# Overflow check and the rows of the last normalisation in the last unit but one, least-used experts last but one

## Chip, core and metric

The kernel runs on one core of a Trainium2 chip. The metric is the device time of one execution in microseconds (us). Engines are named as in the profile: PE (matmul), PEld (weight load of PE), DVE (vector), ACT (scalar), POOL, SP (issues nearly all transfers).

## The reference

Two layers, each a token-mixing part and then a hierarchical mixture of experts, for 256 tokens of width 1024. The part that the change touches, cut to its core:

```python
def hier_moe(h, w_grp, b_grp, w_rt, b_rt, w_gate, w_up, w_down):
    ...
    g_idx = jnp.argmax(grp_logits, axis=-1)
    ...
    top_v, top_i = lax.top_k(sel, TOP_K_IN_GROUP)
    ...
    for e in range(N_EXPERTS):
        a = jax.nn.silu(t @ w_gate[e]) * (t @ w_up[e])
        out = out + combine[:, e:e + 1] * (a @ w_down[e])
...
for l in range(DEPTH):
    ...
    x = layer_norm(DEEPNORM_ALPHA * x + (1 + gt1) * mix, ln1_g[l], ln1_b[l])
    h = x * (1 + sc2) + sh2
    ffn = hier_moe(h, ...)
    x = layer_norm(DEEPNORM_ALPHA * x + (1 + gt2) * ffn, ln2_g[l], ln2_b[l])
```

There are 32 experts of three matrices, each 1024 x 512 in 32-bit floats. Every token goes to two of them. For the inputs used here the reference's router gives these token counts: in layer 0, experts 4 to 31 in falling order 40, 40, 37, 34, 28, 28, 25, 22, 22, 20, 18, 15, 14, 11, 10, 10, 9, 8, 7, 6, 5, 5, 4, 3, 2, 1, 0, 0; in layer 1, 62, 53, 51, 37, 31, 27, 23, 21, 20, 19, 19, 17, 14, 13, 12, 10, 9, 7, 5, 4, 3, 3, 3, 3, 3, 2, 2, 0. So two experts of layer 0 and one of layer 1 have no token.

## The kernel before

**The ring of weights.** All large weights stream through 18 slots of 1 MiB (`RING`). `stream` is the list of loads in the order in which they are used; `pump` issues the next load on SP when one of the 18 is given back, and `done` gives slots back after the matmuls that read them. The order is fixed when the program is written; SP runs ahead of PE by at most 18 slots.

**Places and units.** Experts 0 to 3 stand at places 0 to 3. The other 28 are sorted by their token count on the device, and places 4 to 31 hold them in falling order. Places 0 to 11 get room for 64 tokens each and are worked on in pairs (units 0 to 5), places 12 to 31 get room for 32 each and are worked on in fours (units 6 to 10). A unit of four has 24 loads of 1 MiB: 8 for gate, 8 for up, 8 for down, and within each the four experts alternate. The load of an expert at a place from 4 on has a condition (L176), true where it has at least one token; a load whose condition is false moves no bytes, but holds its slot like any other until PE has passed it. PE does the matmuls of such an expert all the same, on what lies in the slot, and the result is multiplied by zero.

Line 53 makes the units of four in the order 28-31, 24-27, 20-23, 16-19, 12-15, so the four places with fewest tokens are unit 6 and places 12 to 15 are the last unit:

```python
UNITS += [[(p0 + j, 32 * j, 32) for j in range(4)] for p0 in range(NE - 4, FIXED + WIDE - 1, -4)]
```

**A unit on PE** (`experts`, from L1061): gate matmuls (L1117), on every second unit the gathering of the tokens of the next two (`gather`, L1096), up matmuls (L1117), the adding of the unit before to the result `y` in PSUM (`scatter`, L1126), transposes (L1183, L1139), down matmuls (L1205). After the last unit but one (`i == NU - 2`) `add_x` adds the residual to `y` (L1133).

**The overflow check.** `spill` (L1232) handles the case in which an expert has more tokens than its place has room for. Each of the five engines loads the largest overflow from SBUF into a register (L1233) and branches (L1234). Where nothing overflows, as with these inputs, each jumps over the body and its semaphores are stepped on; instructions behind the check that wait for an engine's work wait for that step too (L1234 in the profile). The check stands behind `experts`, at the end of each layer.

**The end of a layer.** Layer 0 is followed by the front of layer 1: `gate_sum` on PE (L387, L479) with the four loads of a gate matrix, `normalise_psum` on DVE and ACT (L546 to L565), transposes of X (L572), and the first section of the projection (L593) with two loads. Layer 1 is followed by the last normalisation (from L1316): PE spreads its scale and shift rows (`fing`, `finb`) over the partitions (L387), ACT copies the scale (L1324), DVE centres and scales (L1337), applies the reciprocal deviation and adds the shift (L1346), and four transfers write the result.

Of the kernel before, what the change touches and what calls it, by code (L numbers as in the profile page):

```python
# [8 lines left out]
F32 = mybir.dt.float32  # L9
BF16 = mybir.dt.bfloat16  # L10
# [17 lines left out]
def kernel(  # L28
# [21 lines left out]

    NR = NE - FIXED
    UNITS = [[(p0 + j, 64 * j, 64) for j in range(2)] for p0 in range(0, FIXED + WIDE, 2)]
    UNITS += [[(p0 + j, 32 * j, 32) for j in range(4)] for p0 in range(NE - 4, FIXED + WIDE - 1, -4)]
    NU = len(UNITS)
    NQ = (NU + 1) // 2
    H = 4
# [1000 lines left out]
        return gc, bc, Xp, posm, rest, places, gsum  # L1057


    def experts(l, gc, bc, Xp, posm, rest, places, gsum, mp):  # L1060
        Gs, Ws, XTs = {}, {}, {}  # L1061
        parts = Xp.bitcast(BF16).rearrange("t k (a c d) -> t a c k d", a=3, c=NTC)
# [46 lines left out]
        wts, eos = {}, {}  # L1109
        st = small.tile([P, NTC, 2, 6], F32, tag="bnst2", name="bnst2")  # L1110

        def proj(i, nm):
# [45 lines left out]
        for i in range(NU):  # L1158
# [69 lines left out]
        ovc, ci = placed["over"]  # L1228
        return y, sts, ovc, ci, gt2


    def spill(l, gc, bc, Xp, ovc, ci, gt, y, sts, mp):  # L1232
        n = nc.values_load(ci[0:1, 0:1], min_val=0, max_val=NT + 32)  # L1233
        with tc.If(n > SLOTS):  # L1234
            for tci in range(NTC):
                for h in range(2):
                    V.tensor_copy(Xn(tci, h), y[tci][h].rearrange("t (p k) -> t p k", k=KD))

            parts = Xp.bitcast(BF16).rearrange("t k (a c d) -> t a c k d", a=3, c=NTC)
            for k in range(KD):  # L1240
                ps = pa.tile([P, 512], F32, tag="a", name="ovh")
                for tci in range(NTC):
                    for a in range(3):
                        T.matmul(ps[:, tci * P:(tci + 1) * P], parts[:, a, tci, k, :], identb,
                                 start=(a == 0), stop=(a == 2))
                S.activation(Xp[:, k, 0:NT], ps[:, 0:NT], AF.Identity, scale=gc[:, k:k + 1], bias=bc[:, k:k + 1])
            with tc.For_i(0, NE, 1) as e:
                for kk in range(KF):
                    f0 = kk * P
                    wg = mp.tile([P, KD, P], F32, tag="XT", name="ovg", bufs=3)  # L1250
                    G.dma_start(wg, w_gate[l][bass.ds(e, 1), :, f0:f0 + P].rearrange(
                        "o (p k) f -> p (o k) f", k=KD))
                    wu = mp.tile([P, KD, P], F32, tag="XT", name="ovu", bufs=3)
                    G.dma_start(wu, w_up[l][bass.ds(e, 1), :, f0:f0 + P].rearrange(
                        "o (p k) f -> p (o k) f", k=KD))
                    wd = mp.tile([P, D], F32, tag="eo", name="ovd", bufs=1)
                    G.dma_start(wd, w_down[l][bass.ds(e, 1), f0:f0 + P, :].rearrange("o p f -> p (o f)"))
                    gps = pa.tile([P, 512], F32, tag="a", name="ovgp")
                    ups = pa.tile([P, 512], F32, tag="a", name="ovup")
                    for ps, w in ((gps, wg), (ups, wu)):  # L1260
                        for k in range(KD):
                            T.matmul(ps[:, 0:NT], w[:, k, :], Xp[:, k, 0:NT], start=(k == 0), stop=(k == KD - 1))
                    aT = mp.tile([P, NT], F32, tag="sg", name="ova", bufs=1)
                    S.activation(aT, gps[:, 0:NT], AF.Silu)
                    V.tensor_tensor(aT, aT, ups[:, 0:NT], op=ALU.mult)
                    for tci in range(NTC):
                        for h in range(2):
                            T.matmul(y[tci][h], aT[:, tci * P:(tci + 1) * P], wd[:, h * 512:(h + 1) * 512],
                                     start=(kk == 0), stop=(kk == KF - 1))
                for tci in range(NTC):  # L1270
                    for h in range(2):
                        t = mp.tile([P, 512], F32, tag="t2", name="ovt")
                        V.tensor_scalar_mul(t, y[tci][h], ovc[:, tci, bass.ds(e, 1)])
                        V.tensor_tensor(t, t, gt[:, h * 512:(h + 1) * 512], op=ALU.mult)
                        xv = Xn(tci, h)
                        V.tensor_tensor(xv, xv, t.rearrange("t (p k) -> t p k", k=KD), op=ALU.add)
            for tci in range(NTC):
                for h in range(2):
                    T.matmul(y[tci][h], ident, Xn(tci, h), start=True, stop=True)
                    V.bn_stats(sts[tci][:, h, :], y[tci][h])  # L1280

    y, sts = None, None
    early, affine = {}, {}
# [2 lines left out]
    for l in range(L):  # L1286
# [24 lines left out]
        fp.stack.close()  # L1311
        mp = moe_pool(l)
        gc, bc, Xp, posm, rest, places, gsum = routing(l, wrs[l], asum, mp)
        y, sts, ovc, ci, gt2 = experts(l, gc, bc, Xp, posm, rest, places, gsum, mp)
        spill(l, gc, bc, Xp, ovc, ci, gt2, y, sts, mp)
        S.preload_act_table_set(LNEXP)  # L1316
        if l + 1 == L:

            fg = mp.tile([P, D], F32, tag="XT", name="fing", bufs=3)
            fb = []  # L1320
            for h in range(2):
# [3 lines left out]
            for h in range(2):  # L1325
# [65 lines left out]
```

## Time and profile before

| | |
|---|---|
| median of 3 executions | 1250.45 us (1249.53 to 1251.41) |
| the profiled execution | 1247.88 us, of which 1246.2 us is the span from first to last instruction |
| mean granted TensorE clock | 0.941 of full |
| PE busy | 1065.2 us, 85% of the span |
| DVE, ACT, POOL busy | 344.8, 172.0, 72.5 us |
| share of the 16 DMA engines taken by SP's queue | 92.7% |
| moved by DMA | 467.62 MB, mean 375 GB/s |

Busy PE is not PE at its peak: matmuls are pipelined and their ends are modelled. Where PE waits for a load, the load is the bound there; where SP waits for PE to give a slot back, PE is. Both occur in this kernel, so the stages have to be read one by one.

### The profile page before, as it was taken

The page shows a single profiled execution, that of the slowest core. Times are in us where ns is not written, and L with a number is a line of the kernel's source. Part 1 is how long each engine was busy: PE and PEld are TensorE (multiplying, and loading weights), DVE is VectorE, ACT ScalarE, POOL GpSimd, SP SyncE. Part 2 cuts the span into 40 slices and gives each one's busy share as a digit, 9 for nine tenths or more (in the row PEclk, how much of TensorE's full clock was granted, in tenths as well). Part 3 has the DMA queues.
Part 4 walks back from the last instruction along what each step waited for, and adds up shares of the span by engine and source line. Part 5 has one row for each costly group of instructions (what it writes and reads, how often), then busy time and mean ns, then how long its engine had stood idle before and what let it go on. Part 6 is the DMA issues. An engine that isn't in the chain of part 4 may idle for free. (4 is left out here: it accounts for less than half of the span.)

```text
span 1246.2 us, 14270 instructions
## 1 busy us (share of the span) xinstructions
PE 1065.2 (85%) x5317; PEld 421.6 (34%) x5320; DVE 344.8 (28%) x801; ACT 172.0 (14%) x403; POOL 72.5 (6%) x52
## 2 busy tenths in 40 slices
PE   5998879899999866788679998989999977677965
PEld 1464434334343311121124653443434221112211
DVE  1386366311121100310034546641112101030103
ACT  1145322101010100000111331310101010000010
POOL 0204520000000000000000301100000000000000
PEclk7999999999999988889989999999999988888897
DMA  9999778899979999999999926889999999999994
GB/s 349 365 411 346 310 297 332 341 403 420 421 312 373 421 422 420 422 421 421 402 395 397 397 70 247 355 343 406 421 421 422 409 421 422 420 422 422 420 409 178
DMA packets 89262, 467.62 MB, mean 375 GB/s; under 512 B 12301, under 2 KB 12817, under 8 KB 40290
## 3 DMA queue, kind: packets, MB, share of 16 engines
q1 hardware_dynamic: 88818, 465.85, 92.7%
q8 instruction: 45, 0.74, 0.2%
q10 hardware_dynamic: 288, 0.52, 0.1%
q0 software_dynamic: 80, 0.26, 0.1%
q14 instruction: 31, 0.25, 0.1%
HBM read 484.43 MB, written 1.05 MB: 390 GB/s over the span
## 5 line engine op out<-in xcount | busy, mean ns | idle before, releaser
L1205 PE MATMUL dps<-w,eaT_moe 128*32 128x512 f32 (+1 forms) x1024 | 199.8, 655 | 39.7 <-DMA w<-in_w_down_dram 30.9
L1117 PE MATMUL up<-w,XT_moe 128*32 128x512 f32 (+1 forms) x1024 | 193.5, 625 | 41.3 <-DMA w<-in_w_up_dram 41.3
L1117 PE MATMUL gate<-w,XT_moe 128*32 128x512 f32 (+1 forms) x1024 | 195.1, 648 | 31.2 <-DMA w<-in_w_gate_dram 31.1
L593 PE MATMUL sec<-w,hT_front 128*128 128x512 f32 x256 | 114.2, 600 | 1.6 <-DVE hT_front L582 1.6
L1205 PEld LDWEIGHTS dps<-w,eaT_moe 128*32 128x32 f32 (+1 forms) x1024 | 53.3, 128 | 169.6 <-issue 100.9
L1117 PEld LDWEIGHTS up<-w,XT_moe 128*32 128x32 f32 (+1 forms) x1024 | 52.2, 124 | 172.3 <-issue 97.4
L1117 PEld LDWEIGHTS gate<-w,XT_moe 128*32 128x32 f32 (+1 forms) x1024 | 53.7, 128 | 167.3 <-issue 107.7
L1171 DVE TENSOR_TENSOR act_moe<-sg_moe,up 128x512 f32<-128x512 f32 x22 | 15.1, 688 | 340.1 <-PE up L1117 340.1
L1211 DVE TENSOR_TENSOR eo_moe<-dps,gt 128x512 f32<-128x512 f32 x44 | 30.4, 691 | 207.0 <-PE dps L1205 207.0
L1126 PE MATMUL y<-eo_moe,wt_moe 128*128 128x512 f32 x176 | 84.9, 607 | 1.6 <-DVE eo_moe L1211 1.6
L1161 ACT ACTIVATE sg_moe<-gate 128x512 f32<-128x512 f32 x22 | 13.1, 597 | 429.2 <-PE gate L1117 429.2
L593 PEld LDWEIGHTS sec<-w,hT_front 128*128 128x128 f32 x256 | 48.0, 192 | 58.5 <-issue 53.3
L1096 PE MATMUL gps<-G_moe,Xp_moe 128*128 128x256 bf16 (+1 forms) x672 | 64.6, 250 | 3.7 <-DVE XT_moe L1102 1.7
L1102 DVE TENSOR_SCALAR XT_moe<-gps,gc,bc 128x128 f32<-128x128 f32 x88 | 30.6, 404 | 126.5 <-PE gps L1096 126.5
L1096 PEld LDWEIGHTS <-Xp_moe 128*128 128x128 bf16 x672 | 53.2, 98 | 21.9 <-issue 13.1
L1141 ACT COPY wt_moe<-wtps 128x256 f32<-128x256 f32 x22 | 8.2, 372 | 287.6 <-PE wtps L1139 287.6
L1126 PEld LDWEIGHTS y<-eo_moe,wt_moe 128*128 128x128 f32 x176 | 30.3, 191 | 43.9 <-issue 40.5
L1105 ACT ACTIVATE XT_moe<-gps,bc,gc 128x128 f32<-128x128 f32 x88 | 33.7, 455 | 42.1 <-PE gps L1096 42.1
L461 POOL TENSOR_TENSOR w<-w,w 128x2048 f32<-128x2048 f32 x7 | 31.6, 4519 | 52.4 <-ACT w L457 41.8
L415 PE MATMUL ada_s<-w,csl 128*32 128x512 f32 x128 | 20.7, 764 | 10.5 <-DMA w<-in_w_ada_dram 10.5
L860 PE MATMUL wo<-w,zu_front 128*128 128x512 f32 x64 | 29.2, 610 | 0.0
L754 PE MATMUL u<-hT_front,w 128*128 128x256 f32 x128 | 28.8, 379 | 0.0
(274 smaller groups left out, 768.6 us busy)
## 6 DMA issues: line engine op xcount, KB each, us to landing
w<-in_w_gate_dram SPq DMA_DIRECT2D x128, 1024.0 KB
w<-in_w_up_dram SPq DMA_DIRECT2D x128, 1024.0 KB
w<-in_w_down_dram SPq DMA_DIRECT2D x120, 1024.0 KB
w<-in_w_ada_dram SPq DMA_DIRECT2D x48, 1024.0 KB
w<-in_w_in_dram SPq DMA_DIRECT2D x20, 1024.0 KB
w<-in_w_out_dram SPq DMA_DIRECT2D x8, 1024.0 KB
w<-in_w_down_dram SPq DMA_DIRECT2D x16, 512.0 KB
xin_front<-in_x_dram SPq DMA_DIRECT2D x2, 512.0 KB
```

Of the source, the lines that this page charges most:

```text
L415: T.matmul(ps[32 * j:32 * j + 32], cs(k), held["ada", l, part, k][:, 0, j * 512:(j + 1) * 512], start=(k == 0), stop=(k == KD - 1))
L461: G.tensor_tensor(acc, acc, w, op=ALU.add)
L593: T.matmul(ps, hT[:, k, tci * P:(tci + 1) * P], held["in", l, s, k // 4][:, k % 4, :], start=(k == 0), stop=(k == KD - 1))
L754: T.matmul(ps[:, 0:NT], held["in", l, U_, k // 4][:, k % 4, g * P:(g + 1) * P], hT[:, k, :], start=(k == 0), stop=(k == KD - 1))
L860: T.matmul(o_ps[tci][h], (cat, zu)[hf][:, kk, tci * P:(tci + 1) * P], w[:, kk, :], start=(hf == 1 and kk == 0), stop=(hf == 0 and kk == 3))
L1096: T.matmul(ps[:, k - kk].rearrange("p j s -> p (j s)"), parts[:, a, tci, k, :], g[:, tci, js[0] * P:(js[-1] + 1) * P], start=(a == 0 and t ...
L1102: V.tensor_scalar(dst, ps[:, k - kk, i, :], gc[:, k:k + 1], bc[:, k:k + 1], op0=ALU.mult, op1=ALU.add)
L1105: S.activation(dst, ps[:, k - kk, i, :], AF.Identity, scale=gc[:, k:k + 1], bias=bc[:, k:k + 1])
L1117: T.matmul(ps[c0:c0 + w], xt[:, k, c0:c0 + w], held[nm, l, place, k // 4][:, k % 4, :], start=(k == 0), stop=(k == KD - 1))
L1126: T.matmul(y[tci][h], wt[:, tci, :], eo[:, h, :], start=(i == 0), stop=(i == NU - 1))
L1205: T.matmul(dps[h][s0:s0 + w], aT[:, kk, s0:s0 + w], held["down", l, place, part][:, kk - ks[0], c0:c0 + 512], start=(kk == 0), stop=(kk == ...
L1211: V.tensor_tensor(eo[:, h, :], dps[h], gt2[:, h * 512:(h + 1) * 512], op=ALU.mult)
```

## The change

Three things are done. The units of four now come in the order 12-15, 16-19, 20-23, 28-31, 24-27. `spill` moves from the end of the layer into the last unit but one, ahead of `add_x`; its body is rewritten so that it adds to the residual X in place of `y`, and it runs only on overflow. The rows of the last normalisation are spread in the last unit but one of layer 1 (`last_rows`), and the shift row is copied to SBUF too; the second preload of the activation table at the layer's end goes.

```diff
-    UNITS += [[(p0 + j, 32 * j, 32) for j in range(4)] for p0 in range(NE - 4, FIXED + WIDE - 1, -4)]
+    FOURS = [[(p0 + j, 32 * j, 32) for j in range(4)] for p0 in range(FIXED + WIDE, NE, 4)]
+    UNITS += FOURS[:-2] + [FOURS[-1], FOURS[-2]]
...
+    def spill(l, gc, bc, Xp, ovc, ci, gt, mp):
+        n = nc.values_load(ci[0:1, 0:1], min_val=0, max_val=NT + 32)
...
+        with tc.If(n > SLOTS):
...
+    def last_rows(l, mp):
+        fg = mp.tile([P, D], F32, tag="XT", name="fing", bufs=3)
+        fb = mp.tile([P, D], F32, tag="Xp", name="finb")
+        for row, r in ((fg, R_LN2G + l), (fb, R_LN2B + l)):
+            for h in range(2):
+                ps = pm.tile([P, 512], F32, tag="m", name="finps")
+                spread(ps, r, h * 512, 512, True, True)
+                (V.tensor_copy if h else S.copy)(row[:, h * 512:(h + 1) * 512], ps)
+        return fg, fb
...
             if i == NU - 2:
+
+                spill(l, gc, bc, Xp, *placed["over"], gt2, mp)
                 add_x()
+                if l + 1 == L:
+                    fin = last_rows(l, mp)
...
-        y, sts, ovc, ci, gt2 = experts(l, gc, bc, Xp, posm, rest, places, gsum, mp)
-        spill(l, gc, bc, Xp, ovc, ci, gt2, y, sts, mp)
-        S.preload_act_table_set(LNEXP)
+        y, sts, fin = experts(l, gc, bc, Xp, posm, rest, places, gsum, mp)
         if l + 1 == L:
 
-            fg = mp.tile([P, D], F32, tag="XT", name="fing", bufs=3)
-            fb = []
-            for h in range(2):
-                ps = pa.tile([P, 512], F32, tag="a", name="fingps")
-                spread(ps, R_LN2G + l, h * 512, 512, True, True)
-                S.copy(fg[:, h * 512:(h + 1) * 512], ps)
-            for h in range(2):
-                fb.append(pm.tile([P, 512], F32, tag="m", name="finbps"))
-                spread(fb[h], R_LN2B + l, h * 512, 512, True, True)
+            fg, fb = fin
...
-                V.scalar_tensor_tensor(o, o, rs[:, tci:tci + 1], fb[h], op0=ALU.mult, op1=ALU.add)
+                V.scalar_tensor_tensor(o, o, rs[:, tci:tci + 1], fb[:, cs], op0=ALU.mult, op1=ALU.add)
```

How this moves instructions is seen at two places. The first is PE at the end of layer 0: the last down matmul and the two last matmuls into `y`, then, in the kernel before, the check with its body (skipped here), and the first matmuls of layer 1 (`gate_g`). Before:

```order
L1205 MATMUL dps<-w_91,eaT_moe_3546 32x512
L1126 MATMUL y_1199<-eo_moe_3553,wt_moe_3551 128x512
L1126 MATMUL y_1201<-eo_moe_3553,wt_moe_3551 128x512
L1233 TENSOR_LOAD ci
L1234 COMPARE_AND_BRANCH
L1244 LDWEIGHTS Xp_moe_1017
...
L1234 UNCONDITIONAL_BRANCH x2
L387 LDWEIGHTS pick_140
L387 MATMUL gate_g_3862<-rw_139,pick_140 32x512
```

The same place with the change:

```order
L1259 MATMUL dps<-w_91,eaT_moe_3789 32x512
L1180 MATMUL y_1199<-eo_moe_3796,wt_moe_3794 128x512
L1180 MATMUL y_1201<-eo_moe_3796,wt_moe_3794 128x512
L388 LDWEIGHTS pick_140
L388 MATMUL gate_g_3861<-rw_139,pick_140 32x512
```

The check has gone from between the two layers. It stands now behind the down matmuls of the last unit but one, on PE ahead of the residual's matmuls and the gate matmuls of the last unit:

```order
L1259 MATMUL dps<-w_95,eaT_moe_3385 32x512
L1062 TENSOR_LOAD ci
L1070 COMPARE_AND_BRANCH
L1076 LDWEIGHTS Xp_moe_1017
...
L1070 UNCONDITIONAL_BRANCH
L1187 MATMUL y_1198<-X,ident 128x512
L1187 MATMUL y_1199<-X,ident 128x512
L1187 MATMUL y_1200<-X,ident 128x512
L1187 MATMUL y_1201<-X,ident 128x512
L1171 MATMUL gate_3694<-w_80,XT_moe_3234 32x512
```

The second place is ACT at the end of layer 1: the end of the check, the copies of the scale row, and the logarithm and exponential that make the reciprocal deviation (`rsy`). Before:

```order
L1247 REGISTER_ALU
L1247 COMPARE_AND_BRANCH
L1247 UNCONDITIONAL_BRANCH
L1234 UNCONDITIONAL_BRANCH x2
L1316 ACT_TABLE_LOAD
L1324 COPY fing_moe_7362<-fingps 128x512 x2
L527 ACTIVATE rsy<-rsv 128x2
L528 ACTIVATE rsy<-rsy 128x2
```

With the change:

```order
L1070 UNCONDITIONAL_BRANCH
L1110 COPY fing_moe_7218<-finps 128x512
L1110 COPY finb_moe_7219<-finps 128x512
L1215 ACTIVATE sg_moe_7273<-gate_7232 128x512
L1195 COPY wt_moe_7326<-wtps 128x256
L1281 ACT_TABLE_LOAD
L528 ACTIVATE rsy<-rsv 128x2
L529 ACTIVATE rsy<-rsy 128x2
```

The copies now stand ahead of the last unit's own two instructions (`sg`, `wt`), and nothing is left between the table and `rsy`. DVE copies the other halves of the two rows at the same place.

## Rows read from the trace of the kernel before

**Rows 1.** The page, GB/s moved in each of 40 slices of 31.2 us

```profile
GB/s 349 365 411 346 310 297 332 341 403 420 421 312 373 421 422 420 422 421 421 402 395 397 397 70 247 355 343 406 421 421 422 409 421 422 420 422 422 420 409 178
```

**Rows 2.** Waits: who waited for what: us in total, times, longest us

```profile
PE dps L1205 <- DMA w<-in_w_down_dram: 30.9, 27, 2.2
```

**Rows 3.** Windows of layer 0: busy, count by engine; PE clock, DMA share, GB/s

```profile
350.00:360.00 10.00, 9.85 (x70) 5.88 (x68) 2.73 (x8) 3.60 (x9) 0.00 (x0) 1.00 1.01 419
360.00:370.00 10.00, 10.00 (x42) 3.98 (x40) 2.14 (x4) 0.37 (x1) 0.00 (x0) 1.00 0.64 246
370.00:380.00 10.00, 10.00 (x74) 3.01 (x74) 1.38 (x2) 0.00 (x0) 0.00 (x0) 1.00 0.43 157
380.00:390.00 10.00, 10.00 (x84) 3.19 (x77) 1.28 (x3) 0.60 (x1) 0.00 (x0) 1.00 0.96 368
...
590.00:600.00 10.00, 8.56 (x48) 2.67 (x44) 0.00 (x0) 0.60 (x1) 0.00 (x0) 1.00 1.01 420
```

**Rows 4.** Timeline of PE in unit 6 of layer 0, and the start of unit 7

```profile
374.56 7.07 PE L1117 MATMUL gate<-w,XT_moe 128*32 128x512 f32 x64
...
392.75 7.07 PE L1205 MATMUL dps<-w,eaT_moe 128*32 128x512 f32 x64
...
405.19 1.04 PE L1117 MATMUL gate<-w,XT_moe 128*32 128x512 f32 x2 [1.10 <-DMA w<-in_w_gate_dram]
```

**Rows 5.** Windows of layer 1 around its unit 6

```profile
960.00:970.00 10.00, 10.00 (x54) 3.32 (x56) 2.51 (x5) 0.37 (x1) 0.00 (x0) 1.00 1.01 397
970.00:980.00 10.00, 10.00 (x99) 2.99 (x92) 0.00 (x0) 0.60 (x1) 0.00 (x0) 1.00 1.00 413
```

**Rows 6.** Timeline of PE in unit 9 of layer 0

```profile
536.40 1.57 PE L1096 MATMUL gps<-G_moe,Xp_moe 128*128 128x128 bf16 x24 [0.15 <-DVE XT_moe L1102]
...
572.77 7.18 PE L1133 MATMUL y<-X,ident 128*128 128x512 f32 x8
```

**Rows 7.** Timeline of all engines where layer 1 follows layer 0

```profile
631.11 1.90 PE L1205 MATMUL dps<-w,eaT_moe 128*32 128x512 f32 x10 [0.30 <-DMA w<-in_w_down_dram]
...
633.79 1.98 PE L1126 MATMUL y<-eo_moe,wt_moe 128*128 128x512 f32 x4 [0.78 <-DVE eo_moe L1211]
...
638.32 0.16 DVE L563 SCALAR_TENSOR_TENSOR nm<-mv,rs 128x1 f32<-128x1 f32 x1
640.60 1.24 ACT L564 ACTIVATE X<-y,nm,rs 128x512 f32<-128x512 f32 x1 [2.95 <-PEq L1234]
...
640.62 0.61 PE L387 MATMUL gate_g<-rw,pick 128*32 128x512 bf16 x2 [4.84 <-PEq L1234]
640.63 4.01 PE L479 MATMUL gate_g<-w,csl 128*32 128x512 f32 x16
...
644.57 1.68 PE L572 MATMUL hTps<-ident,X 128*128 128x128 f32 x8
...
646.17 1.92 PE L479 MATMUL gate_g<-w,csl 128*32 128x512 f32 x16
...
648.03 7.13 PE L593 MATMUL sec<-w,hT_front 128*128 128x512 f32 x16
```

**Rows 8.** Window at the same place, columns as in rows 3

```profile
643.00:644.00 1.00, 1.00 (x8) 0.00 (x0) 0.00 (x0) 0.00 (x0) 0.00 (x0) 0.50 1.10 395
```

**Rows 9.** Timeline of the end of layer 1

```profile
1233.69 0.70 DVE L1226 BATCH_NORM_STATS2 bnst<-y 128x6 f32<-128x512 f32 x1 [0.16 <-PE y L1126]
...
1234.74 0.28 DVE L1330 BATCH_NORM_AGGREGATE fmv<-bnst 128x2 f32<-128x12 f32 x2 [0.36 <-DVEq L1234]
1235.06 0.17 DVE L525 TENSOR_SCALAR rsv<-fmv 128x2 f32<-128x2 f32 x1
...
1236.39 1.07 ACT L1324 COPY fing_moe<-fingps 128x512 f32<-128x512 f32 x2 [20.94 <-PE fingps L387]
...
1237.01 0.75 DVE L1337 SCALAR_TENSOR_TENSOR o_moe<-y,fmv,fing_moe 128x512 f32<-128x512 f32 x1 [1.78 <-ACT fing_moe L1324]
...
1240.28 2.72 DVE L1346 SCALAR_TENSOR_TENSOR o_moe<-o_moe,frs,finbps 128x512 f32<-128x512 f32 x4
```

More of the change, by code (lines that the diff above doesn't have):

```diff
@@ L1057, in routing @@
         return gc, bc, Xp, posm, rest, places, gsum
+    def spill(l, gc, bc, Xp, ovc, ci, gt, mp):
+        n = nc.values_load(ci[0:1, 0:1], min_val=0, max_val=NT + 32)
+        wg = Xp[:, :, NT:NT + P]
+        wu = mp.tile([P, KD, P], F32, tag="XT", name="ovu", bufs=3)
+        wd = [mp.tile([P, 512], F32, tag=tag, name=f"ovd_{tag}", bufs=1) for tag in ("a", "aT")]
+        aT = mp.tile([P, NT], F32, tag="sg", name="ova", bufs=1)
+        t = mp.tile([P, 512], F32, tag="t2", name="ovt")
+        gps, ups = [pa.tile([P, 512], F32, tag="a", name=f"ovp{i}") for i in range(2)]
+        ps = pm.tile([P, 512], F32, tag="m", name="ovps")
+        with tc.If(n > SLOTS):
+            parts = Xp.bitcast(BF16).rearrange("t k (a c d) -> t a c k d", a=3, c=NTC)
+            for k in range(KD):
+                for tci in range(NTC):
+                    for a in range(3):
+                        T.matmul(ps[:, tci * P:(tci + 1) * P], parts[:, a, tci, k, :], identb,
+                                 start=(a == 0), stop=(a == 2))
+                S.activation(Xp[:, k, 0:NT], ps[:, 0:NT], AF.Identity, scale=gc[:, k:k + 1], bias=bc[:, k:k + 1])
+            with tc.For_i(0, NE, 1) as e:
+                for kk in range(KF):
+                    f0 = kk * P
+                    G.dma_start(wg, w_gate[l][bass.ds(e, 1), :, f0:f0 + P].rearrange(
+                        "o (p k) f -> p (o k) f", k=KD))
+                    G.dma_start(wu, w_up[l][bass.ds(e, 1), :, f0:f0 + P].rearrange(
+                        "o (p k) f -> p (o k) f", k=KD))
+                    for h in range(2):
+                        G.dma_start(wd[h], w_down[l][bass.ds(e, 1), f0:f0 + P, h * 512:(h + 1) * 512].rearrange(
+                            "o p f -> p (o f)"))
+                    for pp, w in ((gps, wg), (ups, wu)):
+                        for k in range(KD):
+                            T.matmul(pp[:, 0:NT], w[:, k, :], Xp[:, k, 0:NT], start=(k == 0), stop=(k == KD - 1))
+                    S.activation(aT, gps[:, 0:NT], AF.Silu)
+                    V.tensor_tensor(aT, aT, ups[:, 0:NT], op=ALU.mult)
+                    for tci in range(NTC):
+                        for h in range(2):
+                            T.matmul(ps, aT[:, tci * P:(tci + 1) * P], wd[h], start=True, stop=True)
+                            V.tensor_scalar_mul(t, ps, ovc[:, tci, bass.ds(e, 1)])
+                            V.tensor_tensor(t, t, gt[:, h * 512:(h + 1) * 512], op=ALU.mult)
+                            xv = Xn(tci, h)
+                            V.tensor_tensor(xv, xv, t.rearrange("t (p k) -> t p k", k=KD), op=ALU.add)
@@ L1060, in experts @@
+    def last_rows(l, mp):
+        fg = mp.tile([P, D], F32, tag="XT", name="fing", bufs=3)
+        fb = mp.tile([P, D], F32, tag="Xp", name="finb")
+        for row, r in ((fg, R_LN2G + l), (fb, R_LN2B + l)):
+            for h in range(2):
+                ps = pm.tile([P, 512], F32, tag="m", name="finps")
+                spread(ps, r, h * 512, 512, True, True)
+                (V.tensor_copy if h else S.copy)(row[:, h * 512:(h + 1) * 512], ps)
+        return fg, fb
     def experts(l, gc, bc, Xp, posm, rest, places, gsum, mp):
@@ L1108, in experts @@
         y = [[py.tile([P, 512], F32, tag="s", name=f"y{tci}{h}") for h in range(2)] for tci in range(NTC)]
-        wts, eos = {}, {}
+        wts, eos, fin = {}, {}, None
         st = small.tile([P, NTC, 2, 6], F32, tag="bnst2", name="bnst2")
@@ L1227, in experts @@
         sts = [st[:, tci] for tci in range(NTC)]
[L1228 to L1235, printed above, removed]
-                for h in range(2):
[L1237 to L1266, printed above, removed]
-                        for h in range(2):
[L1268 to L1280, printed above, removed]
@@ L1282 @@
+        return y, sts, fin
     y, sts = None, None
@@ L1313 @@
         gc, bc, Xp, posm, rest, places, gsum = routing(l, wrs[l], asum, mp)
-        y, sts, ovc, ci, gt2 = experts(l, gc, bc, Xp, posm, rest, places, gsum, mp)
-        spill(l, gc, bc, Xp, ovc, ci, gt2, y, sts, mp)
-        S.preload_act_table_set(LNEXP)
+        y, sts, fin = experts(l, gc, bc, Xp, posm, rest, places, gsum, mp)
         if l + 1 == L:
-            fg = mp.tile([P, D], F32, tag="XT", name="fing", bufs=3)
-            fb = []
-            for h in range(2):
-                ps = pa.tile([P, 512], F32, tag="a", name="fingps")
-                spread(ps, R_LN2G + l, h * 512, 512, True, True)
-                S.copy(fg[:, h * 512:(h + 1) * 512], ps)
-            for h in range(2):
-                fb.append(pm.tile([P, 512], F32, tag="m", name="finbps"))
-                spread(fb[h], R_LN2B + l, h * 512, 512, True, True)
+            fg, fb = fin
             mv = small.tile([P, NTC, 2], F32, tag="fmv", name="fmv")
```

## Prediction, before the changed kernel was run

> **What bounds the kernel now.** I read first the GB/s of the 40 slices [rows 1]. The reader is to see a ceiling of 420 to 422 and the slices below it: around slices 12 and 13 (312 and 373, some 343 to 405 us) and in slices 24 to 27. In the ceiling stretches PE waits for loads, for those of down 27 times with 30.9 us in all [rows 2]. So the second half of each layer's experts is bound by the transfers, and what counts there is whether the transfers ever stop. The front of layer 1 (the 70 GB/s slice) is the opposite: the ring is full and PE is the bound. A gain ahead of either kind of stretch is therefore kept only if it moves the resource that binds there, and I take the four places of the change one by one.
>
> Windows of 10 us in layer 0 show the dip closely [rows 3]: 419 GB/s up to 360 us, then 246, 157 and 368, and from 390 us to 600 us, in 21 windows, 417 to 426 (the last is shown). In the dip PE is busy without a break and the granted clock is at its upper level, 2.4 GHz (1.00). PE there is in unit 6 [rows 4]: gate from 374.56, down until 392.75 + 7.07 = 399.8 us, no wait for a load before 405.19. This unit holds the four places with fewest tokens, two of which have none in layer 0. Their 12 loads fill 12 of the 18 slots without giving the transfers anything to do, and PE, which at this time is behind the transfers, has not yet passed them. So the transfers run dry.
>
> **Part 1, the order of the units.** The bytes missing in the dip are (421 - 246) + (421 - 157) + (421 - 368) GB/s over 10 us each, which at 421 GB/s is 4.2 + 6.3 + 1.3 = 11.7 us. By the busy share instead (0.64, 0.43, 0.96 against 1.01) it is 3.7 + 5.7 + 0.5 = 9.9 us. Since the transfers then run at the ceiling until the layer's last load, this is time that layer 0 ends later.
>
> With the change unit 6 is full and the ring holds real loads. Would the stop come back in unit 9? One load takes 1.0486 MB / 421 GB/s = 2.49 us. Unit 9 then has 12 real loads, 29.9 us, and unit 10 has 24, 59.8 us: 89.7 us together. PE needs for a unit of four with all loads there 399.8 - 374.56 = 25.2 us; in unit 9 come the gathering, 2 x 1.57 = 3.1 us, the residual, 7.18 us [rows 6], and the check, 4.84 us [rows 7]: 40.3 us, and 65.5 us for both units. So PE enters unit 9 waiting for loads, ends it 10.4 us late by these sums (40.3 - 29.9), some 20 us with the matmuls that only follow the last loads, and has 24 us of cover until the last load. Twenty us are 8 loads, and SP may run 18 slots ahead, by then all of them loads of unit 10. The transfers do not stop, and I take 11.7 us; lower end 9.9, or nothing in the rival below.
>
> In layer 1 only one expert is empty and the same place loses (421 - 397) + (421 - 413) over 10 us each [rows 5]: 0.8 us, lower end 0.
>
> **Part 2, the check between the layers.** PE's last work of layer 0 is the two matmuls into `y`, over at 633.79 + 1.98 = 635.77 us; the check then holds PE for 4.84 us, to 640.62. ACT and DVE have `nm` at 638.48 but start to normalise X only at 640.60, because they wait for PE's step in the check [rows 7]. So 4.84 us go on PE and 2.12 us on DVE and ACT. But PE, too early, meets the loads. The last load of layer 0 let PE go on at 631.11; at the 395 GB/s shown here [rows 8] one load takes 2.65 us, and between it and the first section stand four loads of the gate matrix, so the section's first load lands at about 631.1 + 5 x 2.65 = 644.4 us. The compute path without the check: X normalised from 638.2 (DVE loses a short wait too) for 1.24 us to 639.5, transposes 1.0 to 1.7 us, the second half of the gate waits for its fourth load (641.7), 1.92 us, done at 642.7 to 643.6. The load comes last: the section starts at 644.4 in place of 648.03, a gain of 3.6 us, on the earlier time base of part 1. From there PE works through the front without waiting for loads, so the gain passes into layer 1's experts, where the ring is refilled by PE's pace.
>
> The clock is the uncertain thing here. Behind the check it is at its lower level, 1.2 GHz (0.50) [rows 8], and 16 matmuls of the gate take 4.01 us; the next 16 take 1.92 us. Without the 4.84 us of idleness it may stay up: that would be worth 2.1 us more, had the loads been there, so the upper end is 4.84 + 2.1 = 6.9 us. PE will instead wait in pieces for loads; if the clock falls during these and the section begins at the lower level, a stretch as long as the one shown costs the 7.13 us section up to 3.6 us, and the lower end is 0. By the Trainium skill ("TensorE: Matmul & The Clock Gate", Part 1) the throttled clock is the default and activity releases it, which would give the upper end's clock where PE stays busy. By that rule the part would be nearer 6.9 us; the transfers keep me at 3.6.
>
> **Part 3, the end of layer 1.** The last statistics end at 1233.69 + 0.70 = 1234.39 us. DVE is ready to centre after `rsv`, 1235.23, and has lost 0.36 us to the check ahead of the aggregate. It then waits for `fing`, copied from 1236.39 on, until 1237.01, and the last scaling starts 3.27 us later at 1240.28 [rows 9]. With rows made in unit 9, `rsv` ends near 1234.9, the first centring starts at about 1234.95, and the logarithm and exponential, which stood behind ACT's copies, fit under it. Gain 1237.01 - 1234.95 = 2.1 us (1.7 if the 0.36 us stay; 2.3 at most). The shift read from SBUF in place of PSUM I leave at no cost.
>
> **Part 4, what is added.** In each layer PE's check stands ahead of the residual and the last unit's gate. Behind it on PE wait the last unit's matmuls, and SP waits for these to give slots back. In layer 1 come four matmuls and four copies for the rows, under 4 us on PE with the waits between them (four copies of 0.54 us, two of them on DVE beside ACT). All this lies in the 24 us of part 1 (39 us in layer 1, whose unit 9 has 18 real loads, 44.8 us), so nothing. Without that cover the check costs 4.84 us in each layer, 9.7 us.
>
> **The sum.** 11.7 + 0.8 + 3.6 + 2.1 = 18.2 us. The profiled execution took 1247.88 us, 1246.2 us of it the span; the median shown is 2.6 us above it, so I subtract from the median: 1250.45 - 18.2 = 1232.3 us.
>
> **Rivals.**
> *The stop returns in unit 9.* The empty experts' slots still fill the ring, now while PE stands in the check and the residual. For it: the cause, 12 empty slots among 24, is the same. Against it: before unit 6 PE never waited for a load, before unit 9 it waits for loads unit after unit, so the slots drain as they are issued. Part 1's 11.7 us would be lost: 1244.0 us.
> *The loads were not the bound, and the front's clock falls.* Only the end of layer 1 and the 0.8 us would remain: 1250.45 - 2.9 = 1247.5 us or a little above. The 21 windows at the ceiling speak against it.
> *Slower: the check stops PE in mid-stream for long.* PE's stop of 4.84 us [rows 7] was measured with the transfers still at about 395 GB/s [rows 8], so the stream alone should not lengthen it. With no cover at all it costs 2 x 4.84 = 9.7 us and gives 1242.0 us. The kernel is slower by more than 0.2% only where the uncovered time passes 18.2 + 2.5 = 20.7 us, some 10.4 us in each layer: with the cover of 24 us that is a stop of nearly 40 us (4.84 + 24 + 10.4), eight times the one shown.
> The Trainium skill ("Runtime: NRT & Kernel Launch", Instruction fetch mechanics) says that a taken branch whose target is not in the fetched window forces a fetch by DMA before execution goes on. By this rule the check stays dear on every engine and DVE, whose skipped body grows, would pay like PE; by the row, DVE paid 0.36 us. Uncovered, the rule gives the 1242.0 us above; covered, it changes nothing.
>
> **Chances.** The forecast 0.76; the stop returns 0.13; next to nothing remains 0.04; the check uncovered 0.07, of which 0.03 slower. Adding ends: best 11.7 + 0.8 + 6.9 + 2.3 = 21.7 gives 1228.7; worst of the forecast 9.9 + 0 + 0 + 1.7 = 11.6 gives 1238.9. To hold 8 in 10 I go from 1228.5 to 1241, into the partial return of the stop. A measurement of this kernel can tell about 0.2%, 2.5 us, from no change. Faster by more than that: 0.92; within it 0.05; slower 0.03.
>
> **What would show it.** Part 1: windows of the changed kernel in layer 0 from some 270 us to the layer's end stay at the ceiling, with no window under 400 before the last 40 us, and the last down load of layer 0 lets PE go on at about 619.4 in place of 631.11. Part 2: PE goes from `y` to the gate without a wait for the check, and the first section waits for its load, and from the last down load's release to the section's first matmul it is 644.4 - 631.1 = 13.3 us in place of 16.9. Part 3: the last scaling starts about 3.8 us after the last statistics in place of 5.9. Wrong would I be if the transfers stop in unit 9, or if PE's waits for the last unit's down loads have gone, which would mean that PE has become the bound.

## The result, and the profile after

With the change the kernel takes 1235.22 us (median; 1234.19 to 1235.47) where before takes 1249.99 us beside it: a ratio of 0.9888, 95% interval 0.9876 to 0.99, that is 14.0 us (12.5 to 15.5) less. Forecast were 18.2 us less, 1232.3 us, with a range of 1228.5 to 1241. The profiled execution took 1234.19 us, its span 1232.6 us.

The GB/s of the 40 slices after, to be held against [rows 1]:

```profile
GB/s 354 365 409 307 294 280 349 347 405 420 422 420 422 421 421 421 421 422 420 400 396 397 388 86 276 348 343 403 422 421 421 420 422 420 421 421 421 420 411 201
```

Slices 12 and 13, which were at 312 and 373, are at the ceiling, and the 409 of layer 1 is 420. The same windows as [rows 3] and [rows 5] (busy and count of PE, PEld, DVE, ACT, POOL; clock, DMA share, GB/s):

```profile
360.00:370.00 10.00, 10.00 (x42) 3.91 (x39) 1.38 (x2) 0.88 (x3) 0.00 (x0) 1.00 1.02 420
370.00:380.00 10.00, 10.00 (x60) 3.16 (x62) 2.15 (x4) 0.37 (x1) 0.00 (x0) 1.00 1.01 420
380.00:390.00 10.00, 8.98 (x82) 2.56 (x74) 0.00 (x0) 0.60 (x1) 0.00 (x0) 1.00 1.01 420
...
550.00:560.00 10.00, 10.00 (x92) 4.05 (x90) 1.42 (x3) 1.34 (x4) 0.00 (x0) 1.00 1.01 419
...
590.00:600.00 10.00, 8.30 (x43) 2.00 (x41) 0.00 (x0) 0.00 (x0) 0.00 (x0) 1.00 1.01 410
...
960.00:970.00 10.00, 9.80 (x82) 2.58 (x74) 0.00 (x0) 0.60 (x1) 0.00 (x0) 1.00 1.02 424
970.00:980.00 10.00, 8.76 (x46) 3.25 (x46) 2.05 (x4) 0.37 (x1) 0.00 (x0) 1.00 1.02 421
```

The stop is gone, and none has come where the unit with the empty experts stands now (550 to 560 us): of the 33 windows from 270 to 600 us the lowest is the 410 shown. PE's timeline there, from the last down matmuls of unit 9 through unit 10 (start, duration, instruction, idle time before it and what ended that), answers to [rows 6]:

```profile
562.67 7.07 PE L1259 MATMUL dps<-w,eaT_moe 128*32 128x512 f32 x64
574.05 7.24 PE L1187 MATMUL y<-X,ident 128*128 128x512 f32 x8 [4.31 <-PEq L1070]
581.22 7.07 PE L1171 MATMUL gate<-w,XT_moe 128*32 128x512 f32 x64
...
598.70 1.04 PE L1171 MATMUL up<-w,XT_moe 128*32 128x512 f32 x2 [1.45 <-DMA w<-in_w_up_dram]
```

The check costs PE 4.31 us here. From 562.67 to 598 us PE then waits for no load, so it is behind the transfers; at 598.70 it waits for one again, so it has caught up. The boundary between the layers, all engines, against [rows 7]:

```profile
622.79 1.90 PE L1259 MATMUL dps<-w,eaT_moe 128*32 128x512 f32 x10 [0.31 <-DMA w<-in_w_down_dram]
...
625.48 1.98 PE L1180 MATMUL y<-eo_moe,wt_moe 128*128 128x512 f32 x4 [0.79 <-DVE eo_moe L1265]
...
627.40 2.10 PE L480 MATMUL gate_g<-w,csl 128*32 128x512 f32 x16
...
629.83 1.21 ACT L565 ACTIVATE X<-y,nm,rs 128x512 f32<-128x512 f32 x1 [0.86 <-DVE nm L564]
631.09 1.09 PE L573 MATMUL hTps<-ident,X 128*128 128x128 f32 x8 [1.59 <-ACT X L565]
...
632.11 2.13 PE L480 MATMUL gate_g<-w,csl 128*32 128x512 f32 x16
...
636.41 7.11 PE L594 MATMUL sec<-w,hT_front 128*128 128x512 f32 x16 [2.17 <-DVE X L566]
```

PE goes from `y` to the gate without a wait, and the gate's first 16 matmuls take 2.10 us in place of 4.01. At 634.24 PE is through the gate and waits 2.17 us for the section's first load. The row names DVE's X, the last thing that ended before, but that is the X of the other 128 tokens, which this section doesn't read; in four of the experiments below the same row names the DMA, and the last experiment moves the load itself. From the last down load's release to the section it is 636.41 - 622.79 = 13.62 us, forecast 13.3, before 16.92. The end of layer 1, against [rows 9]:

```profile
1222.56 0.70 DVE L1284 BATCH_NORM_STATS2 bnst<-y 128x6 f32<-128x512 f32 x1 [0.16 <-PE y L1180]
1223.17 0.33 DVE L1326 BATCH_NORM_AGGREGATE fmv<-bnst 128x2 f32<-128x12 f32 x2
...
1223.61 0.74 DVE L1333 SCALAR_TENSOR_TENSOR o_moe<-y,fmv,fing_moe 128x512 f32<-128x512 f32 x1
...
1226.64 2.74 DVE L1342 SCALAR_TENSOR_TENSOR o_moe<-o_moe,frs,finb_moe 128x512 f32<-128x512 f32 x4
```

From the end of the last statistics to the last scaling it is 1226.64 - 1223.26 = 3.38 us, before 1240.28 - 1234.39 = 5.89, forecast 3.8.

For the experiments I cut each profiled execution at the same marks: unit 0's first `sg` on ACT; the release of the layer's last down load on PE (where PE waits for none there, the layer's last statistics on DVE); the first section of layer 1. In the profile of before unit 0 to last release in layer 0 took 631.11 - 206.94 = 424.17 us, in that of after 622.79 - 209.98 = 412.81 us.

### The profile page after: what moved, and what is told of

It reads as the page before. It is cut to its first block, busy times and chain, and to the rows that moved or that the text cites. A ratio compares the mean times of both kernels' runs of the same rounds, so it can differ in the third digit from the quotient of the medians.

```text
span 1232.6 us, 14266 instructions
## 1 busy us (share of the span) xinstructions
PE 1052.1 (85%) x5318; PEld 417.9 (34%) x5320; DVE 347.1 (28%) x803; ACT 169.5 (14%) x401; POOL 73.2 (6%) x52
## 5 line engine op out<-in xcount | busy, mean ns | idle before, releaser
L1171 PE MATMUL up<-w,XT_moe 128*32 128x512 f32 (+1 forms) x1024 | 188.9, 620 | 33.0 <-DMA w<-in_w_up_dram 33.0
L1171 PE MATMUL gate<-w,XT_moe 128*32 128x512 f32 (+1 forms) x1024 | 187.5, 644 | 26.6 <-DMA w<-in_w_gate_dram 26.6
L1225 DVE TENSOR_TENSOR act_moe<-sg_moe,up 128x512 f32<-128x512 f32 x22 | 15.1, 688 | 315.2 <-PE up L1171 280.5
```

The costliest lines, as they stand in the source:

```text
L1171: T.matmul(ps[c0:c0 + w], xt[:, k, c0:c0 + w], held[nm, l, place, k // 4][:, k % 4, :], start=(k == 0), stop=(k == KD - 1))
```

## The experiments

All are built from the two kernels. Where two medians are told, the first is that of the run and the second that of the kernel before on the same chip.

**The order alone** (before, with the new unit order), and the **check and rows alone** (after, with the old order).

```diff
-    UNITS += [[(p0 + j, 32 * j, 32) for j in range(4)] for p0 in range(NE - 4, FIXED + WIDE - 1, -4)]
+    FOURS = [[(p0 + j, 32 * j, 32) for j in range(4)] for p0 in range(FIXED + WIDE, NE, 4)]
+    UNITS += FOURS[:-2] + [FOURS[-1], FOURS[-2]]
```

> The kernel before with the new order of the units of four alone. Theory (empty loads fill the ring while PE is behind the transfers; at unit 9 PE waits for loads and they drain): no stop around 360 to 390 us, layer 0 ends 11.4 us earlier, the rest as before: about 1250 - 11.4 = 1238.6 us, ratio 0.991. Rival (the gain of layer 0 came from moving the check, the dip being covered): ratio 1.000.

> The changed kernel with the old order of the units (fewest tokens in unit 6): the check and the rows moved alone. Theory: the dip at 360 to 390 us is back; 3.3 us between the layers and 2.5 us at the end stay, 5.8 us in all: about 1244.2 us, ratio 0.9954. Rival (the parts lean on each other: the check is hidden only because the transfers stand ahead with empty experts in unit 9): the check costs 4.3 us in the last unit but one, and the ratio is 0.998 or above.

The order alone: 1238.99 against 1248.94 us, ratio 0.9917 (0.9903 to 0.993); unit 0 to last release 414.17 us. The check and the rows alone: 1246.31 us, 0.9977 (0.9968 to 0.9986), half of what was expected of them. The dip is still there (231 and 154 GB/s from 360 to 380 us), and the section starts 13.65 us after the release. By the ratio alone the rival, 0.998 or above, is as near as the theory; what speaks against it is unit 0 to last release, 424.17 us as in the kernel before, so the check costs nothing where it stands now. What is missing is seen on PE at the boundary of that run:

```profile
643.20 2.14 PE L479 MATMUL gate_g<-w,csl 128*32 128x512 f32 x16
647.52 8.80 PE L593 MATMUL sec<-w,hT_front 128*128 128x512 f32 x16 [2.19 <-DMA w<-in_w_in_dram]
```

The section takes 8.80 us where it takes 7.13 before. With the router's first matmuls (below) that is 2.1 of the 3.2 us missing. The rest may lie at the end of layer 1, which took less in another execution of the kernel before (below); that is not shown. Added up the two parts give 0.83% + 0.23%, near the 1.12% of the whole.

**The changed kernel again**, in two batches.

> The changed kernel once more, to compare the others with on one chip, and to see the start of layer 0, which no edit touches and which stood 3.0 us later in the first profile of the changed kernel than in that of the kernel before (first silu of unit 0 at 209.98 us against 206.94). If that was chance of the granted clock in the opening stretch, it moves by some us from execution to execution and the ratio to before stays at 0.988 to 0.990. If the change had made it later, unit 0 stands near 210 us here too.

> The changed kernel once more, beside the kernel before and the reordered one: 1234 us, ratio 0.988. From the first section to unit 0 of layer 1 either 153.2 us or, where the section starts at the lower clock, 155.0.

The first gave 1234.11 us, 0.9884 (0.9869 to 0.9899); the second 1235.64 against 1248.46 us, 0.989 (0.9871 to 0.9909). In both profiles the section takes 8.80 us, which did not happen in the profile shown above. The windows of the first of them show what happens to the clock:

```profile
634.00:635.00 1.00, 0.52 (x2) 0.31 (x3) 0.39 (x1) 1.00 (x2) 0.00 (x0) 1.00 1.06 389
635.00:636.00 1.00, 1.00 (x3) 0.42 (x2) 0.00 (x0) 0.01 (x1) 0.00 (x0) 0.76 1.05 385
636.00:637.00 1.00, 1.00 (x2) 0.34 (x1) 0.00 (x0) 0.00 (x0) 0.00 (x0) 0.50 1.06 389
637.00:638.00 1.00, 1.00 (x3) 0.46 (x2) 0.00 (x0) 0.00 (x0) 0.00 (x0) 0.50 1.05 387
638.00:639.00 1.00, 1.00 (x3) 0.48 (x2) 0.00 (x0) 0.00 (x0) 0.00 (x0) 0.54 1.05 385
```

The section begins at 634.48 at the upper level, and a microsecond later the granted clock falls to 0.50, 1.2 GHz, and stays there for some 3 us, while PE is busy. What went before on PE are its waits of 0.8, 1.6 and 2.3 us with 7 us of matmuls between them. But nearly the same waits stand in the profile of after (0.79, 1.59 and 2.17 us), whose section takes 7.11 us, so they alone don't decide it. Eight profiles have a wait for the load right ahead of the section: five of them show 8.80 us and three 7.1. In the six others, where PE comes to the section without a wait, it takes 7.13 us each time.

**The kernel before again.**

> The kernel before, unchanged: ratio 1.000 within 0.1%. If the scatter of the start of layer 0 (206 to 210 us in the profiles so far) has nothing to do with the change, this one too lies somewhere between; from the first section to unit 0 of layer 1 it should take 152.9 us, because its gate runs at the lower clock ahead of the section and the section does not.

It gave a ratio of 1.0003 (0.9991 to 1.0016). Start to unit 0 took 207.99 us; over the 14 profiles of this study it lies between 205.9 and 210.0 us for any kernel, so the 3.0 us between the two profiles shown (206.94 and 209.98) are none of the change's doing. Section to unit 0 of layer 1 took 153.0 us as expected. But the end of layer 1 was shorter than in [rows 9]: from the last statistics to the last scaling 1240.88 - 1236.72 = 4.16 us in place of 5.89. The check's branch on PE tells the two apart. Its durations (least, median and greatest of the two layers, ns), first in the profile of before, then in this one:

```profile
L1234 PEldq COMPARE_BRANCH  x2: 3706/4882/6057, 634.4 to 1232.1; - x2
```

```profile
L1234 PEldq COMPARE_BRANCH  x2: 433/3285/6137, 635.0 to 1234.4; - x2
L1234 DVEq COMPARE_BRANCH  x2: 56/64/72, 637.0 to 1236.4; - x2
```

In layer 0 the branch takes PE 6.1 us both times; in layer 1 it took 3.7 us and 0.43 us. On DVE it takes some 60 ns. The run with the order alone, whose check stands at the same place, had 3.67 us there and 5.85 us from the last statistics to the last scaling.

**The rows at the end again**, with the check where the change has it.

```diff
-                if l + 1 == L:
-                    fin = last_rows(l, mp)
...
-            fg, fb = fin
+            fg = mp.tile([P, D], F32, tag="XT", name="fing", bufs=3)
+            fb = []
+            for h in range(2):
+                ps = pa.tile([P, 512], F32, tag="a", name="fingps")
+                spread(ps, R_LN2G + l, h * 512, 512, True, True)
+                S.copy(fg[:, h * 512:(h + 1) * 512], ps)
+            for h in range(2):
+                fb.append(pm.tile([P, 512], F32, tag="m", name="finbps"))
+                spread(fb[h], R_LN2B + l, h * 512, 512, True, True)
```

> The changed kernel with the rows of the last normalisation made at the end of layer 1, as in the kernel before; order and check moved. The end of layer 1 gained 2.5 us. Theory: what was waited for there was the check, which held PE and so the rows behind it; without it PE spreads the rows at once under the last statistics, and 0.2 to 0.5 us are lost against the changed kernel: 1235.5 us. Rival: the rows themselves were the cost, and 1.5 to 2.5 us are lost: 1237 us.

It gave 1233.81 us, 0.9881 (0.9866 to 0.9896): no difference to the changed kernel. The end of its layer 1:

```profile
1218.55 0.70 DVE L1282 BATCH_NORM_STATS2 bnst<-y 128x6 f32<-128x512 f32 x1 [0.16 <-PE y L1180]
1218.56 0.38 PE L388 MATMUL fingps<-rw,pick 128*128 128x512 bf16 x1
1218.76 1.07 ACT L1326 COPY fing_moe<-fingps 128x512 f32<-128x512 f32 x2 [19.06 <-PE y L1180]
...
1219.61 0.75 DVE L1339 SCALAR_TENSOR_TENSOR o_moe<-y,fmv,fing_moe 128x512 f32<-128x512 f32 x1
...
1222.72 2.72 DVE L1348 SCALAR_TENSOR_TENSOR o_moe<-o_moe,frs,finbps 128x512 f32<-128x512 f32 x4
```

PE spreads the row while DVE takes the last statistics, and the copies are done when DVE comes to centre. The last scaling starts 3.47 us after the statistics, 0.09 us later than with rows made early. What the rows waited for in [rows 9] was the check.

**All loads made**, also those of experts without tokens, in both orders.

```diff
-                    cond = {"cond": taken[l, place][0] > NE - 1}
+                    pass
```

> The changed kernel with the condition on the loads taken out: the three experts without a token are loaded like the others, 18 loads more. Theory (only empty loads stop the transfers): 18 x 2.49 = 44.8 us more than the changed kernel, about 1279 us, and the same time with either order of the units. Rival (the order matters for another reason, such as where the check or the residual stands): with the old order it stays some 10 us above this.

> The same with the old order of the units, check and rows moved as in the changed kernel. Theory: no dip at 360 to 390 us any more, and the same time as with the new order to 2 us, about 1279 us. Rival: some 10 us above it, 1289 us.

New order 1282.31 against 1248.55 us, 1.0269 (1.0246 to 1.0293); old order 1278.92 us, 1.0249 (1.023 to 1.0268). The windows of [rows 3] in the old order:

```profile
360.00:370.00 10.00, 10.00 (x42) 3.97 (x40) 2.14 (x4) 0.37 (x1) 0.00 (x0) 1.00 1.01 423
370.00:380.00 10.00, 10.00 (x78) 2.98 (x78) 1.38 (x2) 0.00 (x0) 0.00 (x0) 1.00 1.01 421
380.00:390.00 10.00, 8.65 (x72) 2.28 (x64) 0.00 (x0) 0.60 (x1) 0.00 (x0) 1.00 1.01 419
```

With no empty slots the old order loses nothing: unit 0 to last release takes 443.05 us in it and 444.70 us in the new one, where the orders stand 10.4 us apart with the conditions (below). Against the kernels with conditions these are 19 us and 31 us more; twelve loads more in layer 0 at 2.49 us are 29.9 us, so the old order had some 11 us of stop that they fill. The two medians lie 3.4 us apart, where 2 us at most were expected, and the new order is the slower. The two profiled executions lie 4.8 us apart: 1.3 us in the start, 1.65 us in layer 0, and 1.7 us in a section of 8.80 us against 7.10. Why the new order loses the 1.65 us is not shown.

**Three checks** in place of one, to find the end of the cover.

```diff
-                spill(l, gc, bc, Xp, *placed["over"], gt2, mp)
+                for _ in range(3):
+                    spill(l, gc, bc, Xp, *placed["over"], gt2, mp)
```

> The changed kernel with the check made three times in a row in the last unit but one. One check held PE for 4.3 us in layer 0 and 1.1 us in layer 1. Theory (PE's stop there lies under the last unit's loads): two more per layer, up to 10.8 us of PE's time, change nothing, 1234 us, at most 1 us more. Rival (the check is paid where it stands): 1245 us.

It gave 1237.34 us, 0.9918 (0.9897 to 0.994), 2 to 4 us above the changed kernel, where at most 1 us was expected. Its six executions lie between 1235.24 and 1243.55 us, and the profiled one, 1235.61 us, is among the faster, so the trace shows only a part of the loss. Its section takes 8.80 us, but two of the three profiles of the changed kernel have that too. The stop was longer than I had expected, 19.45 us in layer 0:

```profile
587.03 7.24 PE L1187 MATMUL y<-X,ident 128*128 128x512 f32 x8 [19.45 <-PEq L1070]
594.21 7.07 PE L1171 MATMUL gate<-w,XT_moe 128*32 128x512 f32 x64
...
626.94 0.39 PE L388 MATMUL gate_g<-rw,pick 128*32 128x512 bf16 x2
```

Behind it PE waits for no load until the layer's end, so the cover is used up. Unit 0 to the last statistics of layer 0 took 627.04 - 207.73 = 419.31 us, against 417.52, 418.21 and 418.61 in the three profiles of the changed kernel: 15.1 us more of stop cost 0.7 to 1.8 us. So, as an estimate, one check left 13.3 to 14.4 us of cover, and with its own 4.3 us the whole is some 18 us. In layer 1 the stop was 18.38 us and unit 0 to last release 428.33 us against 428.13: all covered.

**The unit with fewest tokens last.**

```diff
-    UNITS += FOURS[:-2] + [FOURS[-1], FOURS[-2]]
+    UNITS += FOURS
```

> The changed kernel with the four places of fewest tokens as the last unit in place of the last but one. The transfers end as early as in the changed kernel, but in layer 0 the last unit then has only 12 loads, 29.9 us, to cover check 4.3, residual 7.2 and PE's own 25.2 us and more with the adding of the unit before. Theory: PE becomes the bound at the end of layer 0, some 10 us late, and not in layer 1 (18 loads, 44.8 us): 1244 us. Rival (the last load sets the end whatever stands there): 1234 us.

It gave 1241.13 us, 0.9947 (0.9929 to 0.9965); its six executions lie between 1236.71 and 1246.23 us, and the profiled one is the fastest of them. That is nearer the theory's 1244 us than the rival's 1234. The end of layer 0 on PE:

```profile
601.39 7.07 PE L1171 MATMUL gate<-w,XT_moe 128*32 128x512 f32 x64
608.39 3.70 PE L1180 MATMUL y<-eo_moe,wt_moe 128*128 128x512 f32 x8
612.02 7.07 PE L1171 MATMUL up<-w,XT_moe 128*32 128x512 f32 x64
...
638.27 1.92 PE L480 MATMUL gate_g<-w,csl 128*32 128x512 f32 x16
640.12 7.13 PE L594 MATMUL sec<-w,hT_front 128*128 128x512 f32 x16
```

No wait for a load is left, neither in unit 10 nor before the section: the transfers are ahead and PE is the bound. Unit 0 to the last statistics takes 427.52 us, some 9.4 more than with the change, of which the boundary gives back 2.4 (6.47 us from the statistics to the section in place of 8.9), since the section's loads are there.

**The section's loads ahead of half the gate matrix**, a version that the readings above point to.

```diff
-            add_ada(l, "g1", range(4))
+            add_ada(l, "g1", range(2))
             add_in(l, [Q_])
+            add_ada(l, "g1", range(2, 4))
...
-                    gate_sum(l, "g1", 2, gsum1)
                     normalise_psum(1, y_prev[1], sts[1])
                 q0 = section(l, Q_, 0)
+                if l > 0:
+                    gate_sum(l, "g1", 2, gsum1)
```

> The changed kernel, with the two loads of layer 1's first section streamed ahead of the last two loads of the gate matrix, and the second half of the gate's matmuls put behind the section. If the first section was bound by its load, it now starts as soon as X is transposed, 11.5 to 12.5 us after the last down load's release in place of 13.6, or earlier; the gate's last 16 matmuls (2.0 us) then stand in PE's path behind the section, so that the time stays within 1.5 us of the changed kernel. If instead X (the check's remainder, DVE and ACT) was the bound, the section starts 13.6 us after the release as before and the time grows by 2 us. Should the first section run at the lower clock because PE waits in pieces ahead of it, the starts with 155.0 us from section to unit 0 should be gone, since PE waits less there.

> The version with the section's loads first, once more. In its first profile the section started 4.16 us earlier behind the release than in the changed kernel, the gate's second half took 1.9 us of that back, so that the router's matmuls came 2.1 us earlier than in the changed kernel (142.8 us behind the release in place of 144.9) and 3.8 earlier than where the section had started at the lower clock; 1.6 us were then lost because the 32 matmuls of the second gate of layer 1 ran at the lower clock (5.43 us in place of 3.81). If the first is the order's doing and the second is chance, the router again comes 142.8 us behind the release, the section takes 7.1 us, the second gate something between 3.8 and 5.5 us, and the time is 1232 to 1234 us, ratio 0.986 to 0.988.

1232.71 against 1248.46 us, 0.9873 (0.9856 to 0.9889), and in another batch 1232.82 against 1250.13 us, 0.9866 (0.9845 to 0.9886); the changed kernel beside the first took 1235.64 us. PE at the boundary in the first:

```profile
621.42 1.90 PE L1261 MATMUL dps<-w,eaT_moe 128*32 128x512 f32 x10 [0.30 <-DMA w<-in_w_down_dram]
...
629.73 1.09 PE L574 MATMUL hTps<-ident,X 128*128 128x128 f32 x8 [1.60 <-ACT X L566]
630.90 7.13 PE L595 MATMUL sec<-w,hT_front 128*128 128x512 f32 x16
637.96 1.92 PE L481 MATMUL gate_g<-w,csl 128*32 128x512 f32 x16
...
764.25 3.95 PE L946 MATMUL rt<-hT_moe,wr 128*36 128x256 f32 x16 [5.48 <-DVE hT_moe L584]
```

The section starts 9.48 us after the release in place of 13.62 to 13.66, so the load was its bound, and it takes 7.13 us in both profiles. The gate's half that now stands behind it gives 1.92 us back. The router's matmuls (`rt`) start 764.25 - 621.42 = 142.83 us after the release, 142.82 in the second profile; in the profile of the change shown above it is 767.73 - 622.79 = 144.94 us, and where its section ran at the lower level, as in `after_third`, 767.93 - 621.28 = 146.65 us. So this order is worth 2.1 us, or 3.8 where the clock falls. The intervals of the ratios overlap; the marks are what shows the gain. In the first profile these 2.1 us are lost again before unit 0, which comes 166.90 us after the release against 166.93 in the profile of after; 1.6 us of that loss are the next gate's 32 matmuls, which took 5.43 us. In the second they took 3.81, and unit 0 comes after 164.81 us. `after_third` shows the same loss at this place with 4.96 us.

## Why the prediction was right, and where 4 us of it went

**Part 1, right in its cause, 1.3 us too large in layer 0.** Unit 0 to last release takes 424.17, 423.72 and 424.17 us in the three profiles with the old order and the conditions, and 412.81 to 414.40 us, mean 413.64, in the seven that have the new order and are not slowed otherwise. That is 10.4 us; forecast were 11.7 from the missing bytes, and 9.9 was the lower end from the busy share. The truth lies between the two readings of the same rows. One reading needs a limit: at the ceiling PE does not always wait for loads. In the profile of before the windows from 270 to 360 us stand at 418 to 428 GB/s, and PE's first wait for a load in the experts of layer 0 is at 405.19 us. That the empty slots cause the stop is shown by the runs with all loads, where the two orders do not differ in this way. Layer 1's 0.8 us measured 0.6 (mean 428.67 against 428.03 us over the same profiles), no more than the scatter of such a stretch, though its windows are now at the ceiling.

**Part 2, the mechanism right, the clock's share too small.** The check's way out and the section's wait for its load came as forecast: 3.3 us (16.84 to 17.18 with the check between the layers, 13.62 to 13.66 without it), forecast 3.6. The case that the prediction kept for its lower end, a section at the lower level, came in five of eight profiles, at 1.7 us of the possible 3.6. Another 0.1 to 0.5 us, mostly 0.4, went at the router's first matmuls, 3.74 to 3.95 us in place of 3.46 to 3.62, whatever the cause. From section to unit 0 of layer 1 it is 152.9 us on average in the three profiles with the check between the layers, and 154.5 in the eight with a wait ahead of the section: 1.6 us that the sum put at nothing. So the step that failed is the 7.13 us section at the upper level, and the part is worth 1.7 us net. The gate's first 16 matmuls do run faster, 2.10 us in place of 4.01. The Trainium skill says that activity releases the throttle ("TensorE: Matmul & The Clock Gate", Part 1), and here the trace agrees. But PE waited for loads all the same, and in five of eight profiles a low stretch came one step later, in the section.

**Part 3, the size near, the reason not the one that acted.** It measured 2.5 us against the profile of before and the order alone (5.89 and 5.85 to 3.38), forecast 2.1; against the second profile of before, where the branch was short, only 0.8. The prediction put the gain down to rows made in unit 9. The run with the rows at the end shows that they bring 0.09 us; the rest is the check, whose branch stands no longer before PE's spreading. So the size came near by luck and does not speak for the reason given. Whether rows made early would have brought it with the check left at the end was not run.

**Part 4, right.** One check is covered in both layers. The cover in layer 0 was some 18 us, not 24. The sum took 25.2 us for the last unit on PE, from unit 6; with its loads there it takes 626.94 - 594.21 = 32.73 us in the run with three checks, because it also adds its own result to `y` and waits for ACT and DVE with nothing else to do. That is enough for the difference.

**The sum.** 10.4 + 0.6 + 1.7 and between 0.8 and 2.5 give 13.5 to 15.2 us, and the ratios 14.0, 14.5 and 13.7 us. The rival in which the stop returns in unit 9 falls with the windows, and the one in which the loads were not the bound falls with the order alone, 0.9917. The rival of a long stop in mid-stream falls too: three checks stopped PE for 19.45 us and cost 2 to 4 us in all.

**The check's branch.** PE's long branches go together with a transfer of instructions. The profile lists a DMA queue called instruction, and one of its transfers falls into the 6.28 us of PE's branch in layer 0 of the changed kernel (packets, MB, share of the 16 engines in that window):

```profile
q8 instruction: 1, 0.02, 1.1%
```

The same holds in all 14 profiles: each of the 21 branches of PE that took 3.67 us or more has at least one transfer of this queue inside it, the last of which ends some 1.4 us before the branch does, and none of the 11 that took 0.33 to 0.76 us has one. The Trainium skill says that a taken branch whose target is not in the fetched window forces a fetch by DMA before execution goes on ("Runtime: NRT & Kernel Launch", Instruction fetch mechanics), and PE's rows agree, though none of them shows which targets lay in that window. But the check is not dear on every engine: DVE's branch takes some 60 ns.

What stays open is why PE's branch in layer 0 has this transfer inside it in every profile and the one in layer 1 only in some, and what decides between a section of 7.1 and one of 8.8 us where PE waits ahead of it; no run here varied either by itself.

## What to carry to other kernels

In a ring like this one, a transfer that is skipped still holds its buffer until its turn comes. Where the loads are the bound, put such places where PE waits for loads, with a full unit behind them, and neither where PE is behind nor at the very end.

When a stop of PE is taken away, look at what PE waits for next: here a load stood right behind it, and up to the router's matmuls the order of two kinds of loads was worth about as much again as the check's removal.

When a row names what was waited for, ask what that one waited for itself. The rows of the last normalisation looked like the cause and were only behind the check.

## What the runs showed of the hardware that was not expected

- With one check, jumping over its body takes PE's queue some 6 us in layer 0 and between 0.3 and 3.7 us in layer 1, and DVE 0.06 us. With three checks in a row each of the six jumps takes PE 6.2 to 7.0 us, in layer 1 too. PE stands still for less than that where its matmuls still run meanwhile. In the profile of after the branch of layer 0 starts at 567.6 us and takes 6.28, to 573.9, and PE's last matmuls of that stretch end at 569.74: hence the 4.31 us. Of three checks in a row only the first has this cover, so they stopped PE for 19.45 us, more than four times as long.

```profile
L1070 PEldq COMPARE_BRANCH  x2: 581/3430/6278, 567.6 to 1157.3; - x2
```

The same row of the run with three checks:

```profile
L1070 PEldq COMPARE_BRANCH  x6: 6157/6910/7004, 565.5 to 1172.4; - x6
```

- In five profiles the granted clock fell to 0.50 some 0.5 to 1.5 us after PE had gone back to work, not during its wait, and the 16 matmuls of the section took 8.80 us in place of 7.11.
- The start of the kernel, which the change does not touch, varies by 4 us over the 14 profiles (205.9 to 210.0 us to unit 0), and by 3 us over three profiles of the changed kernel alone, about as much as the check's removal from between the layers is worth.
